# Seven experts' results leave by slot and come back by token: DRAM rows and indirect transfers in place of products with one-hot rows

## The chip, the core and the metric

The kernel runs on one core of a Trainium2 chip. The metric is the device time of one execution in microseconds, the median of several runs. The profile names the engines PE (TensorE; PEld is its weight load), DVE (VectorE), ACT (ScalarE), POOL (GpSimd) and SP (SyncE, which here only issues transfers).

## The reference

Two layers over 256 latent tokens of width 1024, with 256 context tokens beside them. Layer 0 is attention and a linear-attention group with a dense feed-forward block; layer 1 is neighbourhood attention and the mixture of experts that this change is about:

```python
def _moe(h, w_router, wg, wu, wd):
    logits = (h @ w_router).astype(jnp.float32)
    top_v, top_i = lax.top_k(logits, TOP_K)              # TOP_K = 2 of 8 experts
    gates = jax.nn.softmax(top_v, axis=-1)
    comb = jnp.sum(gates[..., None] * jax.nn.one_hot(top_i, N_EXPERTS), axis=-2)
    out = jnp.zeros_like(h)
    for e in range(N_EXPERTS):
        out = out + comb[..., e:e + 1] * _swiglu(h, wg[e], wu[e], wd[e])
    return out
...
        x = x + gt2 * ffn(_modulate(_rmsnorm(x, g_norm2[i]), sh2, sc2))
...
    return _rmsnorm(x, g_final)
```

Each expert has three float32 matrices of 1024 x 3584 (3 x 14.68 = 44.04 MB), so eight experts are 352.3 MB of weights for 512 token-expert pairs.

## The kernel before

Layer 0 and the attention of layer 1 take the first 1,040 us; they are not touched. Then the router gives each token two experts, a gate for each, and a rank among the tokens of that expert. Tokens are gathered into slots: an expert has `CAP` = 96 slots (three groups of 32), and a one-hot matrix `oh` (tokens by slots) turns the rows of `xr[2:4]` (the two tiles of 128 tokens) into `X_all` (features by slots), two experts at a time (`gather_pair`, tiles `gx`).

`run_experts` goes through 16 halves, two to an expert (n = 0 to 15; expert n // 2, half b = n % 2). A half is: `up`, the gate product `pg` (8 loads of 896 KB, 192 matmul instructions), then the up product `pu` (the same), then ACT's SiLU and DVE's product and transpose into `eT`; and behind that `down`, the product `py` of the half before (7 loads of 1 MB, 336 instructions). Every weight goes by `load_raw` on SP's queue into a ring of 13 buffers; SP may issue a load when PE has read the buffer out. `mm_quarters` spreads a product over four groups of 32 columns of PE, so that four matmuls run beside each other.

In the middle of each `pu` (at k = 4) `run_experts` calls `middle(n)`, which does two things. For an expert whose last `down` is over, that is at n = 3, 5, ... 15, it calls `scatter`: ACT and DVE copy `py` out of PSUM into `yF`, which is split into `yhi` and `ylo`; PE multiplies both by `ohT` (slots by tokens) into `sc`, eight matmuls of 96 x 512; DVE multiplies by the token's gate and by `gate2`, and POOL (DVE for the last expert) adds to `xr`. Then `between(n)` runs: at even n `route_slots` transposes the expert's one-hot matrix into `ohT` (two PE transposes and an ACT copy), at n = 2, 6, 10 the next pair is gathered, and at n = 0 `route_gates` makes the gates and counts tokens per expert. Expert 7's `scatter` stands behind everything, followed by `finish_out`, the final norm. Program order on each engine comes from a scheduler that follows priorities; weight loads stand 500 steps ahead.

Of the kernel before, what the change touches and what calls it, by code (L numbers as in the profile page):

```python
# [7 lines left out]
F32 = mybir.dt.float32  # L8
F32R = mybir.dt.float32r
I32 = mybir.dt.int32  # L10
AF = mybir.ActivationFunctionType
ALU = mybir.AluOpType
AX = mybir.AxisListType
# [3 lines left out]
P = 128  # L17
D = 1024
KT = 8
# [6 lines left out]
NE = 8  # L26

GROUPS = 3
CAP = 32 * GROUPS
# [10 lines left out]
C_W8 = C_WIN + 64  # L40
# [49 lines left out]
def kernel(ctx, tc, x, c, ctx_in, c_ctx, w_mod, b_mod, g_norm1, g_norm2, w_in_ab, g_q, g_k,  # L90
# [3 lines left out]
    nc = tc.nc  # L94
# [4 lines left out]
    def new_pool(stack, name, bufs=1, side="left", **kw):  # L99
        return stack.enter_context(tc.tile_pool(name=name, bufs=bufs, side=side, reuse_waits="tile", **kw))  # L100

    small = ctx.enter_context(tc.tile_pool(name="small", bufs=4))
    dram = ctx.enter_context(tc.tile_pool(name="dram", bufs=1, space=DRAM))
# [12 lines left out]
    def bankA(name):  # L116
        return banks["p"].tile([P, 512], F32, tag="p", name=name)

    def bankB(name, tag="x"):
        return banks[tag].tile([P, 512], F32, tag=tag, name=name)  # L120
# [23 lines left out]
    def cc(o, n=P):  # L144
        return cst[:, o - P:o - P + n] if o < C_KEEP else cst0[:, o - C_KEEP:o - C_KEEP + n]
# [13 lines left out]
    def pick(tags, n):  # L159
        seq = [t for t in tags for _ in range(t[2])]  # L160
        return seq[n % len(seq)]
# [66 lines left out]
    featp = new_pool(ctx, "featp", side="right")  # L228
# [104 lines left out]
    def gate_rows(pool, l, cond, v, tag, bufs, bank="x"):  # L333
        g = pool.tile([P, D], F32, tag=tag, bufs=bufs, name=f"gate{l}_{cond}_{v}")
        for h in range(2):
            q = 2 * v + h
            i, j = q // 4, q % 4
            ps = bankB(f"gate_ps{l}_{cond}_{v}_{h}", bank)
            sel = ident[:, 32 * j + cond:32 * j + cond + 1].to_broadcast([P, P])
            nc.tensor.matmul(ps, sel, m_sb[l][:, i, :], start=True, stop=True)  # L340
            nc.scalar.copy(g[:, h * 512:(h + 1) * 512], ps)
        return g
# [171 lines left out]
    with ahead(PREP):  # L514
        nz = state["n"]
        state["n"] += 1
        pool, tag, bufs = pick(raw_tags, state["r"])
# [4 lines left out]
        pool, tag, bufs = pick(hi_tags, nz)  # L522
        wz_hi = pool.tile([P, KT, P], F32R, tag=tag, bufs=bufs, name="wz_hi")
        pool, tag, bufs = pick(lo_tags, nz)
# [43 lines left out]
    for d in range(2):  # L568
        tri = cc(C_TF if d == 0 else C_TB)
        for p in range(2):  # L570
            ps = bankB(f"bc{d}_{p}")
            for t in range(NT):
                o = d * 256 + p * P
                nc.tensor.matmul(ps[:, t * P:(t + 1) * P], la[:, t, o:o + P], tri, start=True, stop=True)
            e1 = t1p.tile([P, 512], F32, tag="gt", bufs=3, name=f"e1_{d}_{p}")
            e2 = t1p.tile([P, 512], F32, tag="gt", bufs=3, name=f"e2_{d}_{p}")
# [151 lines left out]
    xr = [(resc if t < 2 else resid).tile([P, D], F32, name=f"xr{t}") for t in range(NT)]  # L728
# [228 lines left out]
    for g in range(NG):  # L957
# [27 lines left out]
        for t in range(NT):  # L985
            for half in range(2):
                hs = slice(half * 512, half * 512 + 512)
# [10 lines left out]
    for s, cond in streams:  # L998
        both = fmp.tile([P, 2, D], F32, tag=f"fT{s}", bufs=2, name=f"xc{s}")
# [29 lines left out]
    gate2 = gate_rows(resid, 1, 0, 5, "gate", 1, bank="s")  # L1029
# [97 lines left out]
    mop = new_pool(mo, "mop", side="right")  # L1127
# [6 lines left out]
    rank = mop.tile([P, 2, NE], F32, name="rank")  # L1134
    cnt_i = mop.tile([1, 1], I32, name="cnt_i")
    oh, ohT = {}, {}
# [4 lines left out]
    tops, scales = [], []  # L1141
# [3 lines left out]
    def rt(name, n=NE):  # L1145
        return mop.tile([P, n], F32, name=name)
# [78 lines left out]
    def route_rows():  # L1225

        for t in range(2):
            for h in range(2):
                hs = slice(h * 512, h * 512 + 512)
                nc.scalar.mul(xs_hi[t][:, hs], xr[2 + t][:, hs], scales[t])  # L1230
                scaled = exp_.tile([P, 512], F32, tag="ytmp", bufs=2, name=f"scaled{t}_{h}")
                nc.scalar.mul(scaled, xr[2 + t][:, hs], scales[t])
                nc.gpsimd.tensor_tensor(xs_lo[t][:, hs], scaled, xs_hi[t][:, hs].bitcast(F32), op=ALU.subtract)

    def one_hot(ep):

        oh[ep] = mop.tile([P, 2, 2, CAP], F32R, tag="oh", bufs=2, name=f"oh{ep}")
        for e in range(2):
            for t in range(2):
                nc.vector.tensor_scalar(oh[ep][:, t, e, :], iota, rank[:, t, 2 * ep + e:2 * ep + e + 1],  # L1240
                                        sel[:, t, 2 * ep + e:2 * ep + e + 1], op0=ALU.is_equal, op1=ALU.mult)

    def route_exp():
        for t in range(2):
# [3 lines left out]
            nc.scalar.activation(e2, e2, AF.Exp)  # L1248
            tops[t] += [e2]

    def route_gates():
        for t in range(2):
            m1, o1, m2, o2, e2 = tops[t]
            den, g1 = rt(f"den_{t}", 1), rt(f"g1_{t}", 1)
            nc.vector.tensor_scalar_add(den, e2, 1.0)
            nc.vector.reciprocal(g1, den)
            nc.vector.tensor_tensor(e2, e2, g1, op=ALU.mult)
            nc.vector.tensor_scalar_mul(o1, o1, g1)
            nc.vector.scalar_tensor_tensor(comb[:, t, :], o2, e2, o1, op0=ALU.mult, op1=ALU.add)
        ps = bankB("cnt_ps")  # L1260
        for t in range(2):
            nc.tensor.matmul(ps[:, 0:NE], cc(C_ONE), sel[:, t, :], start=(t == 0), stop=(t == 1))
        cmax = rt("cmax", 1)
        nc.vector.tensor_reduce(cmax, ps[:, 0:NE], axis=AX.X, op=ALU.max)
        nc.vector.tensor_copy(cnt_i, cmax[0:1, :])

    def slot_rows(ohs, name):

        tp = bankA(f"ohT_ps{name}").bitcast(F32R)
        for t in range(2):  # L1270
            nc.tensor.transpose(out=tp[0:CAP, t * P:(t + 1) * P], in_=ohs[t], identity=ident_r)
        rows_ = mop.tile([CAP, 256], F32R, tag="ohT", bufs=2, name=f"ohT{name}")
        nc.scalar.copy(rows_, tp[0:CAP, 0:256].bitcast(F32))
        return rows_

    def route_slots(e):
        ohT[e] = slot_rows([oh[e // 2][:, t, e % 2, :] for t in range(2)], f"{e}")
# [10 lines left out]
    NB, BW = 2, 1792  # L1288
# [28 lines left out]
    class Expert:  # L1317
# [41 lines left out]
        def down(self, b, eTs):  # L1359
# [4 lines left out]
            for i in range(ni):  # L1364
                with ahead(PREP):
                    wd = load_raw(self.wd[b * ni + i], [P, 2, D])
                for j in range(2):

                    begin = b == 0 and i == 0 and j == 0
                    for s in range(GROUPS):  # L1370
                        mm_quarters(self.py[s], eTs[s][:, 2 * i + j, :], wd[:, j].rearrange("p (q x) -> p q x", q=4),
                                    begin and s % 2 == 0, b == NB - 1 and i == ni - 1 and j == 1)

        def scatter(self):
            name, pool = self.name, self.pool
            ohT_e = self.ohT_e()
            yF = y_room()
            hi, lo = [pool.tile([CAP, D], F32R, tag=f"y{p}", bufs=1, name=f"y{p}_{name}") for p in ("hi", "lo")]
            pss = {}
            for h in range(2):  # L1380
                hs = slice(h * 512, h * 512 + 512)
                for n, (s, q) in enumerate((s, q) for s in range(GROUPS) for q in (2 * h, 2 * h + 1)):
                    (nc.vector.tensor_copy if n % 2 else nc.scalar.copy)(  # L1383
                        yF[32 * s:32 * s + 32, q * 256:(q + 1) * 256], self.py[s][32 * q:32 * q + 32])
                nc.scalar.copy(hi[:, hs], yF[:, hs])
                nc.vector.tensor_tensor(lo[:, hs], yF[:, hs], hi[:, hs].bitcast(F32), op=ALU.subtract)
                for t in range(2):
                    ps = bankA(f"sc_{name}_{h}_{t}")
                    for n, part in enumerate((hi, lo)):
                        nc.tensor.matmul(ps, ohT_e[:, t * P:(t + 1) * P], part[:, hs], start=(n == 0), stop=(n == 1))  # L1390
                    tmp = pool.tile([P, 512], F32, tag="ytmp", bufs=2, name=f"ytmp_{name}_{h}_{t}")
                    nc.vector.scalar_tensor_tensor(tmp, ps, self.gate(t), gate2[:, hs], op0=ALU.mult, op1=ALU.mult)  # L1392
                    (nc.vector if self.last else nc.gpsimd).tensor_tensor(xr[2 + t][:, hs], xr[2 + t][:, hs], tmp,  # L1393
                                                                          op=ALU.add)

    def run_experts(experts, between=lambda n: None):

# [23 lines left out]
    rooms = {}  # L1421

    def X_room(ep):

        if "X" not in rooms:
            rooms["X"] = featp.tile([P, 2, KT, 2 * CAP], F32, tag="f0", bufs=1, name="X_all")
        return rooms["X"][:, ep % 2]

    def y_room():

        if "y" not in rooms:
            both = featp.tile([P, D], F32, tag="f1", bufs=1, name="yF")
            rooms["y"] = both
        return rooms["y"][0:CAP]

    def gather_pair(ep, tags):
        rows, ohs = ((xs_hi, xs_lo), oh[ep]) if ep else ((xr[2:4],), oh_r)
# [3 lines left out]
    def between(n):  # L1441

        ep, i = divmod(n, 2 * NB)
        if n == 0:
            with tc.issue_after(critical["gathered"]), tc.issue_after(critical["one-hot"]):
                one_hot(0)
                route_gates()
                route_rows()
        if n % NB == 0:
            route_slots(n // NB)  # L1450
        if i == 1 and ep + 1 < NE // 2:
            with tc.issue_after(critical["one-hot"]):
                one_hot(ep + 1)
        if i == 2 and ep + 1 < NE // 2:
            gather_pair(ep + 1, "p")
# [98 lines left out]
```

## Time and profile before

| | |
|---|---|
| median of 3 runs | 1993.11 us (1990.57 to 1993.86) |
| the profiled execution's own time | 1991.23 us |
| its span, first to last instruction | 1989.3 us |
| PE busy | 1926.8 us (97%) |
| DVE, ACT, POOL busy | 741.6, 448.0, 142.7 us |
| moved by the DMA engines | 493.32 MB, mean 248 GB/s |

The span is what the views of the profile show; 1.9 us of the profiled time lie around it. A line number is that of the kernel before.

### The profile page before, as it was taken

What the parts mean: (1) busy time and instruction counts of PE and PEld (TensorE: products, weight loads), DVE (VectorE), ACT (ScalarE), POOL (GpSimd) and SP (SyncE); (2) the same over time, 40 slices, a digit from 0 to 9 for tenths busy, and PEclk for the clock granted to TensorE, in tenths of its full rate; (3) what the DMA queues carried; (4) which work ended last, traced back from release to release, by engine and by line L of the source; (5) the groups of instructions that cost most, each with busy time, mean ns of one, the idle gap of its engine ahead of it and who ended that gap; (6) DMA issues with size and microseconds to landing.
All of it is one profiled execution on the core that took longest, in us unless ns stands there. A gap on an engine that the chain in (4) does not pass through costs nothing.

```text
span 1989.3 us, 37121 instructions
## 1 busy us (share of the span) xinstructions
PE 1926.8 (97%) x16627; PEld 1177.0 (59%) x16627; DVE 741.6 (37%) x1190; ACT 448.0 (23%) x732; POOL 142.7 (7%) x177
## 2 busy tenths in 40 slices
PE   5999999899999999999999999999999999999996
PEld 3666676787878877777764444545444344544433
DVE  3246588866556435536772101011110101111022
ACT  4232165422222222336542010010100010010001
POOL 1101010100000000104211000001010100101010
PEclk8999999999999999999999999999999999999998
DMA  8624120634536244233239999999999999999991
GB/s 335 218 104 170 48 82 14 235 133 170 201 132 217 85 129 136 73 99 94 74 129 368 399 394 386 379 405 379 385 387 402 392 388 362 377 409 385 407 398 40
DMA packets 125213, 493.32 MB, mean 248 GB/s; under 512 B 10696, under 2 KB 58120, under 8 KB 104568
## 3 DMA queue, kind: packets, MB, share of 16 engines
q1 hardware_dynamic: 114096, 481.04, 63.6%
q10 hardware_dynamic: 8648, 6.48, 1.1%
q0 software_dynamic: 2304, 3.36, 0.8%
q8 instruction: 132, 2.16, 0.4%
q14 instruction: 33, 0.27, 0.0%
HBM read 486.13 MB, written 4.72 MB: 247 GB/s over the span
## 4 chain that ended last, share of the span: by engine, by line
PE 93%; DVE 2%; DMA 2%; ACT 1%; issue 1%; POOL 0%; SPq 0%; POOLq 0%; ACTq 0%; DVEq 0%
PE pu_e L1315 15%; PE pg_e L1315 15%; PE py_e L1315 15%; PE pf_fu L481 3%; PE pf_fu L482 3%; PE pf_fu L483 3%; PE pf_fg L481 3%; PE pf_fg L482 3%; PE pf_fg L483 3%; PE fd L217 3%; PE fd L215 2%; PE fd L216 2%; PE sc_e L1390 1%; PE mod_ps L254 1%; PE o_c L860 1%
## 5 line engine op out<-in xcount | busy, mean ns | idle before, releaser
L1315 PE MATMUL pu_e<-raw,X_all 128*32 128x448 f32 x3072 | 306.1, 540 | 0.0
L1315 PE MATMUL py_e<-raw,eT_e 128*32 128x256 f32 x5376 | 296.5, 379 | 0.0
L1315 PE MATMUL pg_e<-raw,X_all 128*32 128x448 f32 x3024 | 291.4, 539 | 0.0
L1315 PEld LDWEIGHTS py_e<-raw,eT_e 128*32 128x32 f32 x5376 | 190.5, 110 | 105.0 <-issue 5.1
L1315 PEld LDWEIGHTS pg_e<-raw,X_all 128*32 128x32 f32 x3024 | 100.0, 110 | 181.2 <-issue 175.5
L1315 PEld LDWEIGHTS pu_e<-raw,X_all 128*32 128x32 f32 x3072 | 98.5, 110 | 182.4 <-issue 178.8
L204 DVE TENSOR_TENSOR wlo<-raw,whi 128x2048 fp32r<-128x2048 f32 (+1 forms) x69 | 153.2, 2227 | 125.2 <-ACT whi L202 124.8
L202 ACT CAST whi<-raw 128x2048 fp32r<-128x2048 f32 (+1 forms) x73 | 135.1, 1859 | 267.0 <-PE fd L217 113.3
L1352 DVE TENSOR_TENSOR m_sb<-m_sb,pu_e 128x448 f32<-128x448 f32 x48 | 27.9, 604 | 393.5 <-PE pu_e L1315 393.4
L1348 ACT ACTIVATE m_sb<-pg_e 128x448 f32<-128x448 f32 x48 | 26.1, 544 | 512.8 <-PE pg_e L1315 512.8
L481 PE MATMUL pf_fu<-f_hi,whi 128*128 128x512 f32 (+1 forms) x240 | 91.5, 381 | 3.4 <-ACT whi L202 3.4
L1393 POOL TENSOR_TENSOR xr<-xr,ytmp_e 128x512 f32<-128x512 f32 x28 | 35.2, 1277 | 822.5 <-DVE ytmp_e L1392 822.5
L481 PE MATMUL pf_fg<-f_hi,whi 128*128 128x512 f32 (+1 forms) x240 | 93.0, 388 | 0.6 <-ACT whi L202 0.6
L483 PE MATMUL pf_fg<-f_hi,wlo 128*128 128x512 f32 (+1 forms) x240 | 91.6, 382 | 1.8 <-DVE wlo L204 1.8
L482 PE MATMUL pf_fg<-f_lo,whi 128*128 128x512 f32 (+1 forms) x240 | 92.2, 384 | 0.7 <-DVE f_lo L381 0.7
L482 PE MATMUL pf_fu<-f_lo,whi 128*128 128x512 f32 (+1 forms) x240 | 91.7, 382 | 0.0
L483 PE MATMUL pf_fu<-f_hi,wlo 128*128 128x512 f32 (+1 forms) x240 | 91.5, 381 | 0.0
L217 PE MATMUL fd<-whi,fT 128*128 128x512 f32 x224 | 88.3, 395 | 0.0
L215 PE MATMUL fd<-whi,fT 128*128 128x512 f32 x224 | 88.0, 393 | 0.0
L216 PE MATMUL fd<-wlo,fT 128*128 128x512 f32 x224 | 88.0, 393 | 0.0
L1392 DVE SCALAR_TENSOR_TENSOR ytmp_e<-sc_e,comb,gate 128x512 f32<-128x512 f32 x32 | 23.6, 750 | 165.3 <-PE sc_e L1390 160.5
L1383 ACT COPY yF<-py_e 32x256 f32<-32x256 f32 x48 | 17.4, 363 | 265.9 <-PE py_e L1315 257.6
(375 smaller groups left out, 2676.6 us busy)
## 6 DMA issues: line engine op xcount, KB each, us to landing
raw<-in_w_moe_up_dram SPq DMA_DIRECT2D x128, 896.0 KB, 6.4
raw<-in_w_moe_down_dram SPq DMA_DIRECT2D x112, 1024.0 KB, 8.0
raw<-in_w_moe_gate_dram SPq DMA_DIRECT2D x126, 896.0 KB, 7.8
raw<-in_w_mod_dram SPq DMA_DIRECT2D x48, 1024.0 KB, 4.9
raw<-in_w_ff_gate_dram SPq DMA_DIRECT2D x14, 1024.0 KB, 5.6
raw<-in_w_ff_up_dram SPq DMA_DIRECT2D x14, 1024.0 KB, 5.4
raw<-in_w_ff_down_dram SPq DMA_DIRECT2D x14, 1024.0 KB, 4.9
raw<-in_w_in_c_dram SPq DMA_DIRECT2D x12, 1024.0 KB, 5.2
```

The costliest lines, as they stand in the source:

```text
L202: nc.scalar.copy(hi[:, c], raw[:, c])
L204: low.tensor_tensor(lo[:, c], raw[:, c], hi[:, c].bitcast(F32), op=ALU.subtract)
L215: nc.tensor.matmul(ps, ah, bh, start=start, stop=False)
L216: nc.tensor.matmul(ps, ah, bl, start=False, stop=False)
L217: nc.tensor.matmul(ps, al, bh, start=False, stop=stop)
L481: nc.tensor.matmul(ps, wh[:, k, ws], hh[:, k, ts], start=(k == 0), stop=False)
L482: nc.tensor.matmul(ps, wh[:, k, ws], hl[:, k, ts], start=False, stop=False)
L483: nc.tensor.matmul(ps, wl[:, k, ws], hh[:, k, ts], start=False, stop=(k == KT - 1))
L1315: nc.tensor.matmul(out[32 * q:32 * q + 32], lhsT, rhs[:, q], start=start, stop=stop, skip_group_check=True)
L1348: nc.scalar.activation(g, ps[s][:, 0:QW], AF.Silu)
L1352: nc.vector.tensor_tensor(gs[s], gs[s], ps[s][:, 0:QW], op=ALU.mult)
L1393: (nc.vector if self.last else nc.gpsimd).tensor_tensor(xr[2 + t][:, hs], xr[2 + t][:, hs], tmp, op=ALU.add)
```

## The change

Experts 0 to 6 no longer multiply by `ohT`. `store` copies `py` into `yF` (one of two places, in turn), multiplies by `gate2`, and ACT issues a transfer of the 96 rows of 4 KB to their slots in a DRAM tensor `y_d` of 7 x 96 rows and one row of zeros. `route_back`, called from `route_gates`, works out for each token and each of its two choices the row in `y_d` (the zero row for expert 7 and for a token beyond the 96 slots). At n = 15 `add_back` has POOL issue four indirect transfers, each of 128 rows of 4 KB, one for each token tile and choice, into free parts of the tiles of `yF` and `X_all`, and DVE adds them to `xr` with the gates. Expert 7 keeps the product with `ohT`. `ohT` is made for expert 7 alone.

```diff
+    NY = (NE - 1) * CAP
+    y_d = dram.tile([NY + 1, D], F32, name="y_d")
+    y_idx = mop.tile([P, 2, 2], I32, name="y_idx")
+    def route_back():
+        zero = mop.tile([8, P], F32, name="zero")
+        nc.gpsimd.memset(zero, 0.0)
+        nc.scalar.dma_start(y_d[NY:NY + 1, :].rearrange("o (a b) -> (o a) b", a=8), zero)
+        for t in range(2):
+            v, u = rt(f"v{t}"), rt(f"u{t}")
+            nc.vector.scalar_tensor_tensor(v, cc(C_W8, 8), -float(CAP), rank[:, t, :], op0=ALU.mult, op1=ALU.add)
+            nc.vector.tensor_scalar_add(v, v, float(8 * CAP - NY))
+            nc.vector.scalar_tensor_tensor(v, rank[:, t, :], float(CAP), v, op0=ALU.is_lt, op1=ALU.mult)
+            nc.vector.memset(v[:, NE - 1:NE], 0.0)
+            for k in range(2):
+                i = rt(f"i{t}_{k}", 1)
+                nc.vector.tensor_tensor(u, v, tops[t][1 + 2 * k], op=ALU.mult)
+                nc.vector.tensor_reduce(i, u, axis=AX.X, op=ALU.add)
+                nc.vector.tensor_scalar_add(y_idx[:, t, k:k + 1], i, float(NY))
+    def add_back():
+        rooms_ = [rooms["y"][:, 2], rooms["y"][:, 3], rooms["X4"][:, 0:D], rooms["X4"][:, 3 * D:4 * D]]
+        for t in range(2):
+            for k in range(2):
+                nc.gpsimd.indirect_dma_start(rooms_[2 * t + k], None, y_d,
+                                             bass.IndirectOffsetOnAxis(ap=y_idx[:, t, k:k + 1], axis=0))
+        for t in range(2):
+            m1, o1, m2, o2, e2, g1 = tops[t]
+            for h in range(2):
+                hs = slice(h * 512, h * 512 + 512)
+                for k, g in enumerate((g1, e2)):
+                    xh = xr[2 + t][:, hs]
+                    nc.vector.scalar_tensor_tensor(xh, rooms_[2 * t + k][:, hs], g, xh, op0=ALU.mult, op1=ALU.add)
     def route_gates():
+        route_back()
...
+        def store(self):
+            n = int(self.name[1:])
+            yF = y_room(n % 2)
+            for h in range(2):
+                hs = slice(h * 512, h * 512 + 512)
+                for i, (s, q) in enumerate((s, q) for s in range(GROUPS) for q in (2 * h, 2 * h + 1)):
+                    (nc.vector.tensor_copy if i % 2 else nc.scalar.copy)(
+                        yF[32 * s:32 * s + 32, q * 256:(q + 1) * 256], self.py[s][32 * q:32 * q + 32])
+                nc.vector.tensor_tensor(yF[:, hs], yF[:, hs], gate2[0:CAP, hs], op=ALU.mult)
+            nc.scalar.dma_start(y_d[n * CAP:n * CAP + CAP, :], yF)
         def scatter(self):
+            if not self.last:
+                return self.store()
...
-        if n % NB == 0:
-            route_slots(n // NB)
+        if n == (NE - 1) * NB:
+            route_slots(NE - 1)
+        if n == NE * NB - 1:
+            add_back()
```

The scheduler's order shows what this does to the engines. The first place is PE in the middle of expert 1's second half (n = 3), where expert 0 is scattered; `pu_e_1` is the up product, `sc` the product with `ohT`. Before:

```order
L1315 MATMUL pu_e_1_9146<-raw_9190,X_all 32x448 x4
L1315 MATMUL pu_e_1_9147<-raw_9190,X_all 32x448 x4
L1390 MATMUL sc_e_0_0_9215<-yhi_e_9205,ohT_8052 128x512 [waits Activation_49]
L1390 MATMUL sc_e_0_0_9215<-ylo_e_9206,ohT_8052 128x512 [waits DVE_49]
L1390 MATMUL sc_e_0_1_9221<-yhi_e_9205,ohT_8052 128x512 [waits Activation_49]
L1390 MATMUL sc_e_0_1_9221<-ylo_e_9206,ohT_8052 128x512
L1390 MATMUL sc_e_1_0_9235<-yhi_e_9205,ohT_8052 128x512 [waits Activation_49]
L1390 MATMUL sc_e_1_0_9235<-ylo_e_9206,ohT_8052 128x512 [waits DVE_49]
L1315 MATMUL pu_e_1_9145<-raw_9247,X_all 32x448 [waits DMAHW3_49]
L1390 MATMUL sc_e_1_1_9241<-yhi_e_9205,ohT_8052 128x512 [waits DVE_49]
L1390 MATMUL sc_e_1_1_9241<-ylo_e_9206,ohT_8052 128x512
L1315 MATMUL pu_e_1_9145<-raw_9247,X_all 32x448 x3
```

And in the changed kernel, from the same weight tile on:

```order
L1354 MATMUL pu_e_1_9169<-raw_9199,X_all 32x448 x4
L1354 MATMUL pu_e_1_9170<-raw_9199,X_all 32x448 x4
L1354 MATMUL pu_e_1_9168<-raw_9213,X_all 32x448 [waits DMAHW4_49]
L1354 MATMUL pu_e_1_9168<-raw_9213,X_all 32x448 x3
L1354 MATMUL pu_e_1_9169<-raw_9213,X_all 32x448 x4
```

The eight products are gone and the up product runs through; the next weight tile comes on semaphore lane 4 in place of 3, since the store to `y_d` has taken lane 3.

The second place is DVE in the last half (n = 15), between the end of expert 6 and the product `m_sb` that makes expert 7's last `eT`. Before:

```order
L1386 TENSOR_TENSOR ylo_e_14694<-yF,yhi_e_14693 96x512 [waits Activation_49]
L1392 SCALAR_TENSOR_TENSOR ytmp_e_0_0_14706<-sc_e_0_0_14703,comb,gate_0_5_6114 128x512 [waits PE_49,Pool_49]
L1392 SCALAR_TENSOR_TENSOR ytmp_e_0_1_14712<-sc_e_0_1_14709,comb,gate_0_5_6114 128x512 [waits PE_49,Pool_49]
L1392 SCALAR_TENSOR_TENSOR ytmp_e_1_0_14726<-sc_e_1_0_14723,comb,gate_0_5_6114 128x512 [waits PE_49,Pool_49]
L1392 SCALAR_TENSOR_TENSOR ytmp_e_1_1_14732<-sc_e_1_1_14729,comb,gate_0_5_6114 128x512 [waits PE_49,Pool_49]
L1352 TENSOR_TENSOR m_sb_1588<-m_sb_1588,pu_e_1_14634 128x448 [waits PE_49,Activation_49]
```

In the changed kernel:

```order
L1422 TENSOR_TENSOR yF<-yF,gate_0_5_6114 96x512 [waits DVE_49]
L1286 SCALAR_TENSOR_TENSOR xr_1594<-yF,g_0_8047,xr_1594 128x512 [waits DMASW0_49]
L1286 SCALAR_TENSOR_TENSOR xr_1594<-yF,g_0_8047,xr_1594 128x512
L1286 SCALAR_TENSOR_TENSOR xr_1594<-yF,e_0_7831,xr_1594 128x512 [waits DMASW1_49,DVE_49]
L1286 SCALAR_TENSOR_TENSOR xr_1594<-yF,e_0_7831,xr_1594 128x512 [waits DVE_49]
L1286 SCALAR_TENSOR_TENSOR xr_1595<-X_all,g_1_8054,xr_1595 128x512 [waits DMASW2_49]
L1286 SCALAR_TENSOR_TENSOR xr_1595<-X_all,g_1_8054,xr_1595 128x512
L1286 SCALAR_TENSOR_TENSOR xr_1595<-X_all,e_1_7834,xr_1595 128x512 [waits DMASW3_49,DVE_49]
L1286 SCALAR_TENSOR_TENSOR xr_1595<-X_all,e_1_7834,xr_1595 128x512 [waits DVE_49]
L1391 TENSOR_TENSOR m_sb_1588<-m_sb_1588,pu_e_1_14470 128x448 [waits PE_49,Activation_49]
```

DVE now waits for the four indirect transfers (the lanes DMASW0 to DMASW3) ahead of the work that makes `eT`. The third place is POOL's issue of them, behind the last work that POOL has from the start of the expert stage:

```order
L1233 TENSOR_TENSOR xs_lo_7644<-scaled_1_8079,xs_hi_7642 128x512 [waits Activation_49]
L1278 DMA yF<-y_d,y_idx 128x1024 [waits DMAHW4_49,DMAHW3_49,DMAHW5_49,DMAHW2_49,DMAHW6_49,DMAHW1_49,DMAHW7_49,DVE_49,PE_49]
L1278 DMA yF<-y_d,y_idx 128x1024 [waits DVE_49]
L1278 DMA X_all<-y_d,y_idx 128x1024 [waits PE_49,Activation_49]
L1278 DMA X_all<-y_d,y_idx 128x1024 [waits DVE_49]
L349 TENSOR_TENSOR rs_nf_fin<-ms_nf_fin,mhalf 128x1 [waits DVE_49] x2
```

The 28 additions to `xr` that stood here on POOL are gone; the first transfer waits for the stores of all seven experts, the third also for PE, which reads `X_all`.

## Rows read from the trace of the kernel before

**Rows 1.** The page: busy us by engine, and DMA busy tenths in 40 slices.

```profile
PE 1926.8 (97%) x16627; PEld 1177.0 (59%) x16627; DVE 741.6 (37%) x1190; ACT 448.0 (23%) x732; POOL 142.7 (7%) x177
...
DMA  8624120634536244233239999999999999999991
```

**Rows 2.** First and last matmuls of the expert stage, line 1315 (ns, then start us).

```profile
L1315 PE MATMUL py_e<-raw,eT_e x5376: 379/379/379, 1133.4 to 1967.7; 128*32 128x256 f32 x200
...
L1315 PE MATMUL pg_e<-first,X_all x48: 539/539/563, 1060.0 to 1064.1; 128*32 128x448 f32 x48
```

**Rows 3.** The chain in order of time, halves n = 4 and 5 (start, us, what).

```profile
1267.89 0.20 PE pg_e L1315
...
1268.11 17.66 PE pg_e L1315 x187
...
1295.17 0.27 PE ohT_ps L1271 x2
...
1304.59 18.13 PE py_e L1315 x336
1322.72 18.04 PE pg_e L1315 x192
...
1380.19 4.87 PE pg_e L1315 x49
```

**Rows 4.** The chain in order of time, half n = 9.

```profile
1550.50 18.04 PE pg_e L1315 x192
1568.54 0.67 PE sc_e L1390 x2
...
1608.25 18.04 PE pg_e L1315 x192
```

**Rows 5.** Stretches of the expert stage: busy time by engine, clock, DMA.

```profile
core 0: us, PE busy (x) PEld busy (x) DVE busy (x) ACT busy (x) POOL busy (x), PEclk, DMA share, GB/s
...
1452.00:1465.00 13.00, 13.00 (x144) 4.42 (x136) 0.00 (x0) 1.63 (x3) 0.00 (x0) 1.00 1.01 423
...
1100.00:1930.00 830.00, 830.00 (x10592) 373.21 (x10588) 96.89 (x177) 61.05 (x132) 35.25 (x28) 1.00 1.00 390
```

**Rows 6.** What SP's queue waited for in the expert stage (total us, times, longest).

```profile
SPq L169 <- PE pu_e L1315: 263.4, 121, 5.9
SPq L169 <- PE pg_e L1315: 243.5, 124, 16.7
SPq L169 <- PE py_e L1315: 215.5, 99, 2.2
```

**Rows 7.** What PE's weight loads waited for: the costliest wait for a transfer.

```profile
PEld pu_e L1315 <- DMA raw<-in_w_moe_down_dram: 2.0, 8, 0.2
```

**Rows 8.** SP's timeline: when the seven loads used from 1304.59 are issued.

```profile
1277.18 13.86 SPq L169 DMA_DIRECT2D raw<-in_w_moe_down_dram  x7
```

**Rows 9.** DMA issues by line: KB each, median us to landing.

```profile
raw<-in_w_moe_down_dram SPq DMA_DIRECT2D x112, 1024.0 KB, 8.0
...
bias<-rb_d POOLq DMA_DIRECT2D x32, 96.0 KB, 2.9
...
out_dram<-z_fin ACTq DMA_DIRECT2D x2, 256.0 KB, 2.5
```

**Rows 10.** DVE's timeline in the last half, n = 15.

```profile
1892.20 1.77 DVE L1383 COPY yF<-py_e 32x256 f32<-32x256 f32 x4 [16.11 <-ACT yF L1383]
...
1896.77 0.69 DVE L1386 TENSOR_TENSOR ylo_e<-yF,yhi_e 96x512 fp32r<-96x512 f32 x1 [0.69 <-ACT yhi_e L1385]
...
1919.67 0.75 DVE L1392 SCALAR_TENSOR_TENSOR ytmp_e<-sc_e,comb,gate 128x512 f32<-128x512 f32 x1 [2.30 <-PE sc_e L1390]
...
1930.41 0.62 DVE L1352 TENSOR_TENSOR m_sb<-m_sb,pu_e 128x448 f32<-128x448 f32 x1 [6.93 <-PE pu_e L1315]
...
1932.67 1.16 DVE L1354 STREAM_TRANSPOSE eT_e<-m_sb 128x448 f32<-128x448 f32 x2
```

**Rows 11.** The chain in order of time, the end of the expert stage.

```profile
1931.78 35.87 PE py_e L1315 x664
```

More of the change, by code (lines that the diff above doesn't have):

```diff
@@ L1257, in route_gates @@
             nc.vector.tensor_tensor(e2, e2, g1, op=ALU.mult)
+            tops[t] += [g1]
             nc.vector.tensor_scalar_mul(o1, o1, g1)
@@ L1271, in slot_rows @@
             nc.tensor.transpose(out=tp[0:CAP, t * P:(t + 1) * P], in_=ohs[t], identity=ident_r)
-        rows_ = mop.tile([CAP, 256], F32R, tag="ohT", bufs=2, name=f"ohT{name}")
+        rows_ = mop.tile([CAP, 256], F32R, tag="ohT", bufs=1, name=f"ohT{name}")
         nc.scalar.copy(rows_, tp[0:CAP, 0:256].bitcast(F32))
@@ L1392, in scatter @@
                     nc.vector.scalar_tensor_tensor(tmp, ps, self.gate(t), gate2[:, hs], op0=ALU.mult, op1=ALU.mult)
-                    (nc.vector if self.last else nc.gpsimd).tensor_tensor(xr[2 + t][:, hs], xr[2 + t][:, hs], tmp,
-                                                                          op=ALU.add)
+                    nc.vector.tensor_tensor(xr[2 + t][:, hs], xr[2 + t][:, hs], tmp, op=ALU.add)
     def run_experts(experts, between=lambda n: None):
@@ L1425, in X_room, with y_room @@
         if "X" not in rooms:
-            rooms["X"] = featp.tile([P, 2, KT, 2 * CAP], F32, tag="f0", bufs=1, name="X_all")
+            rooms["X4"] = featp.tile([P, 4 * D], F32, tag="f0", bufs=1, name="X_all")
+            rooms["X"] = rooms["X4"][:, 0:4 * KT * CAP].rearrange("p (a k n) -> p a k n", a=2, k=KT)
         return rooms["X"][:, ep % 2]
-    def y_room():
+    def y_room(i=0):
         if "y" not in rooms:
-            both = featp.tile([P, D], F32, tag="f1", bufs=1, name="yF")
-            rooms["y"] = both
-        return rooms["y"][0:CAP]
+            rooms["y"] = featp.tile([P, 4, D], F32, tag="f1", bufs=1, name="yF")
+        return rooms["y"][0:CAP, i]
     def gather_pair(ep, tags):
```

## The prediction

> **What bounds the kernel now.** I read the page first. PE is busy for 1926.8 us of the span [rows 1], so time can only go where PE gets less to do, unless something stands close behind it. Something does: the DMA tenths read 9 through the whole second half [rows 1]. That half is the expert stage, which the change touches, from PE's first `pg` at 1060.0 to its last `py` at 1967.7 [rows 2]: 907.7 us. So the question is whether PE or the weight stream paces it.
>
> The stretches say both are full: from 1100 to 1930 PE is busy for 830.00 of 830 us at the full clock and the DMA share is 1.00, at 390 GB/s [rows 5]. A share of 1.00 does not yet make a limit, for in the stretch from 1452 to 1465 us, where SP issues faster than usual, a share of 1.01 stands beside 423 GB/s [rows 5]; 390 is what is asked of the DMA engines, not what they can do. Two more views tell the same. SP's queue spent 722 us waiting for PE to read buffers out (263.4, 243.5 and 215.5) [rows 6], while PE's costliest wait for a weight load is 2.0 us in all, in eight pieces [rows 7]. And the seven loads whose first use is at 1304.59 [rows 3] are issued from 1277.18 on [rows 8]: 27.4 us ahead, of which landing takes about 8.0 [rows 9], so that a weight lies ready for some 19 us. PE paces the stage; the stream follows it with 19 us in hand.
>
> **What a half costs without anything in its middle.** The chain gives 18.04 us for 192 gate matmuls and 18.13 us for 336 `py` [rows 3]; the up product has as many matmuls of the same shape as the gate product, 18.04. A bare half is 54.21 us, and 16 of them 867.4. The stage takes 907.7, so 40.3 us are for what stands between: scatters, `ohT`, the gathers, the count.
>
> **Removed: seven scatters.** Half n = 5 holds one and nothing else. It runs from 1322.72 to 1380.19 [rows 3], 57.47 us. At such a seam two gate matmuls of the next half run before the last `py` (one of the two pieces stands at 1267.89); at 18.04/192 = 0.094 us each they belong to the other half: 57.28, or 3.07 over the bare half. Half n = 9 runs from 1550.50 to 1608.25 [rows 4], 57.75: 3.54 over. There the scheduler put the products one or two at a time between up matmuls ([rows 4] shows two `sc` in front), and each change of shape costs. In the chain n = 3, 5, 7 and 11 have the first form, n = 9, 13 and 15 the second: 4 x 3.07 + 3 x 3.54 = 22.9 us. Bounds: the first form throughout gives 21.5, the second 24.8.
>
> **Removed: seven transpositions into `ohT`.** Half n = 4 has one alone: from 1268.11, less 0.19 for its two early gate matmuls, to 1322.72 [rows 3] is 54.80, 0.59 over. At n = 8 and 12 it is the same. At n = 0, 2, 6 and 10 a count or a gather stands beside it and pays for the change of shape anyway; there only its own 0.27 [rows 3] goes. 3 x 0.59 + 4 x 0.27 = 2.9. Together 25.8 us. The rest of the 40.3, 14.5 us, is left to what stays (three gathers, the count, expert 7's `ohT`).
>
> **Removed elsewhere.** 28 additions on POOL, 28 gated products on DVE, the splits into `yhi` and `ylo` on ACT and DVE: none is on the path, since PE is busy throughout [rows 5]. I price them at nothing. Expert 7's own scatter and the final norm, the time after 1967.7, are unchanged.
>
> **Added at the start: `route_back`.** Twenty DVE operations of a few elements, a memset, one small transfer that ACT issues. They stand under expert 0's gate product, when DVE has nothing PE waits for before the first half's end. Nothing.
>
> **Added: seven stores.** ACT issues one after DVE's second product with `gate2`; behind it on ACT is the SiLU of the same half. At n = 15 the copies run from 1892.20 and the second 96 x 512 operation that now becomes that product starts at 1896.77 and takes 0.69 [rows 10], so the store goes at about 1897.5. The SiLU needs the gate product, which lasts 18.04 us from about 1892: 13 us of cover. The store takes a semaphore lane from the weight loads; SP waits for it eight loads later, some 18 us after. Landing: between 2.5 us (256 KB, ACT's queue) and 8.0 (1024 KB under the weight stream) [rows 9]. Hidden either way.
>
> **Added: traffic.** Seven stores of 0.39 MB and four fetches of 0.52 MB are 4.85 MB. From 1100 to 1930 the engines moved 390 x 0.830 = 323.7 MB; nearly all of the change's gain lies there, so the same work and 4.85 MB more would have to pass in about 805 us: 408 GB/s, against 423 seen [rows 5]. The 19 us in hand are worth 7.8 MB at that rate, so PE starts to wait only if the sustained rate falls below (328.5 - 7.8)/805 = 398 GB/s. Below that, each per cent costs 8 us. I take 423, the row that shows a full queue, and so nothing.
>
> **Added: the fetch and eight additions at n = 15.** POOL's first fetch waits for the last store, landed between 1900 and 1905.5. A fetch of 512 KB has no row; its bounds are 2.9 us (96 KB on POOL's queue) and 8.0 (1024 KB) [rows 9], so four, one after the other at worst, end between 1912 and 1938; if the last two wait for the up matmuls ahead of them on PE, they still start by about 1920. Eight additions of 128 x 512 at 0.75 each [rows 10] are 6 us: done between 1918 and 1944. DVE has the product `m_sb` next, which ran at 1930.41, its transposes ending at 1933.8 [rows 10]. PE uses that `eT` only after expert 7's first `py`: 1931.78 + 18.13 [rows 11, 3], less the 3.54 that this half loses, 1946.4. DVE must therefore begin by 1943. Against the early bound there are 25 us to spare, against the late one 1 us is missing. I take the early side (nearer in size and with overlap between fetches): nothing.
>
> **The sum.** 25.8 us off the profiled execution's 1991.23 gives 1965.4; off the median 1993.11, which is 1.9 higher, 1967.3. I say 1967, and for this case 1963 to 1971 (scatters 21.5 to 24.8, transpositions 1.9 to 4.1, and the 3.3 us spread of the runs).
>
> **Rivals.** (1) *The weight stream was the limit all along.* Then PE's gaps closed nothing, since the share of 1.00 says the engines are full; the 4.85 MB come on top at 390 GB/s, 12.4 us: **2005**, slower. For it: the share [rows 5]. Against it: 423 GB/s and the waits of [rows 6, 7]. It decides if 390 is a limit, that is if SP stops waiting for PE.
> The Trainium skill speaks for this rival: "DMA: Bandwidth & Descriptors", Specifications, gives a limit of about 358 GB/s for HBM per core. By it 328.5 MB need 918 us, 88 more than before, and the kernel would end near 2081. This trace does not agree, with 390 GB/s over 830 us [rows 5].
> (2) *The stream becomes the limit once PE is quicker*, since stores between loads cost more than their bytes. At a sustained 390 after the change, (328.5 - 7.8)/390 = 822 us in place of 805: 17 of the 25.8 us are given back, **1985**. At 386 all of them, and below that the kernel is slower than before. For it: 408 of 423 leaves 3.5%. Against it: a small store every 108 us is 0.9% of the bytes.
> (3) *The fetch is late and DVE holds back the last `eT`.* PE then stands still before expert 7's last `py`. Each us past 1943 costs one; at 10 us past, **1977**. It outweighs the gain only if the additions end after 1969, 71 us after the store is issued.
> (4) *The gaps go only in part*: PE's removed products leave a wait in their place, as PSUM banks now turn over in another order and a gate product meets a SiLU or eviction that it used to follow. Half the gain, **1980**. Against it: evictions are done 5 us after `py` [rows 10], half a half ahead of need.
>
> **Chances.** Forecast 0.80; rival (1) 0.04, (2) 0.07, (3) 0.05, (4) 0.04. The range for 8 in 10 is 1962 to 1977: the forecast's own range with a us on the low side, and upwards to the mild ends of (2), (3) and (4). 0.2%, or 4 us, is about what a measurement of this kernel tells from no change. Rivals (2) and (3) reach no change or worse in a third of their weight, (1) is slower: faster 0.91, same 0.03, slower 0.06.
>
> **What would show it.** In the changed kernel's chain a half with nothing in it takes 54.2 us, seven more of them than now; SP still waits mostly for PE; the DMA rate from 1100 to the end of the stage is about 405 GB/s; PE has no wait for a transfer above a few us; DVE's additions end before 1943 on the old scale (about 1918 on the new); and the tail after the last `py` is as long as before. I am wrong if PE waits for weights in growing pieces towards the end, if it stands before the last `py`, or if bare halves take longer than 54.2.

## The result and the profile after

The changed kernel takes 1966.57 us (median of 4 runs, 1965.11 to 1969.37) against 1992.38 for the kernel before in the same call: a ratio of 0.9872, with a 95% interval of 0.986 to 0.9885 (estimated from all runs; it need not be the quotient of the two medians to the last digit). The profiled execution took 1966.8 us, with a span of 1964.9.

The page of the changed kernel, as [rows 1]: busy us by engine, and the DMA busy tenths.

```profile
PE 1903.2 (97%) x16557; PEld 1171.3 (60%) x16557; DVE 726.8 (37%) x1190; ACT 437.5 (22%) x711; POOL 111.6 (6%) x154
...
DMA  9634020645436343123337999999999999999994
```

PE lost 23.6 of its busy us and is still the engine that never rests; every DMA slice that lies wholly in the expert stage still reads 9. The chain in order of time, halves n = 4 and 5, a piece of n = 6, and the end, as [rows 3, 11]:

```profile
1264.43 18.04 PE pg_e L1354 x192
...
1318.64 18.04 PE pg_e L1354 x192
...
1372.85 18.04 PE pg_e L1354 x192
1390.89 2.25 PE pu_e L1354 x24
1393.43 2.39 PE pu_e L1354 x24
1396.11 2.39 PE pu_e L1354 x24
1398.79 2.39 PE pu_e L1354 x24
1401.18 3.42 PE gx L1342 x29
...
1431.88 18.04 PE pg_e L1354 x192
...
1907.37 35.93 PE py_e L1354 x666
```

Half n = 4 (1264.43 to 1318.64) and half n = 5 (to 1372.85) last 54.21 us each: bare, as the prediction priced them. The last `py` instruction begins at 1943.3, and the span ends 21.6 us later, as before (1989.3 less 1967.7).

SP's queue, what it waited for most between 1060 and 1945 us (us in total, times, longest), as [rows 6]; then the weight loads of PE, as [rows 7]:

```profile
SPq L169 <- PE pu_e L1354: 228.2, 118, 5.8
SPq L169 <- PE py_e L1354: 190.6, 92, 2.2
SPq L169 <- PE pg_e L1354: 188.7, 103, 14.4
SPq L169 <- DMA y_d<-yF: 63.8, 6, 14.8
SPq L169 <- DMA raw<-in_w_moe_down_dram: 22.6, 18, 2.9
```
```profile
PEld pg_e L1354 <- DMA raw<-in_w_moe_up_dram: 2.9, 12, 0.2
```

SP now waits for the stores too: 63.8 us in six pieces, up to 14.8. PE's own worst wait for a weight is still 0.2 us. The DMA issues by line (KB each, median us to landing), as [rows 9]:

```profile
raw<-in_w_moe_down_dram SPq DMA_DIRECT2D x112, 1024.0 KB, 12.9
...
y_d<-yF ACTq DMA_DIRECT2D x7, 384.0 KB, 5.1
...
yF<-y_d,y_idx POOLq DMA_INDIRECT x2, 10.5
X_all<-y_d,y_idx POOLq DMA_INDIRECT x2, 15.3
```

And DVE's timeline in the last half, as [rows 10]:

```profile
1891.52 1.42 DVE L1286 SCALAR_TENSOR_TENSOR xr<-yF,g,xr 128x512 f32<-128x512 f32 x2 [15.98 <-DMA yF<-y_d,y_idx]
...
1902.94 1.41 DVE L1286 SCALAR_TENSOR_TENSOR xr<-X_all,e,xr 128x512 f32<-128x512 f32 x2 [3.08 <-DMA X_all<-y_d,y_idx]
1906.06 0.62 DVE L1391 TENSOR_TENSOR m_sb<-m_sb,pu_e 128x448 f32<-128x448 f32 x1 [1.71 <-PE pu_e L1354]
```

The additions end at 1904.35, and `m_sb` behind them waits for PE, not for them.

### The profile page after: what moved, and what is told of

Same layout as the page of the kernel before. It is cut to its first block, busy times and chain, and to the rows that moved or that the text cites. A ratio compares the mean times of both kernels' runs of the same rounds, so it can differ in the third digit from the quotient of the medians.

```text
span 1964.9 us, 36952 instructions
## 1 busy us (share of the span) xinstructions
PE 1903.2 (97%) x16557; PEld 1171.3 (60%) x16557; DVE 726.8 (37%) x1190; ACT 437.5 (22%) x711; POOL 111.6 (6%) x154
## 4 chain that ended last, share of the span: by engine, by line
PE 93%; DVE 2%; DMA 2%; ACT 2%; issue 1%; POOL 0%; SPq 0%; ACTq 0%; POOLq 0%; DVEq 0%
PE pu_e L1354 15%; PE py_e L1354 15%; PE pg_e L1354 15%; PE pf_fu L481 3%; PE pf_fu L482 3%; PE pf_fu L483 3%; PE pf_fg L481 3%; PE pf_fg L482 3%; PE pf_fg L483 3%; PE fd L217 3%; PE fd L216 3%; PE fd L215 3%; PE mod_ps L254 1%; PE o_c L860 1%; PE gx L1342 1%
## 5 line engine op out<-in xcount | busy, mean ns | idle before, releaser
L1354 PE MATMUL pu_e<-raw,X_all 128*32 128x448 f32 x3072 | 296.2, 539 | 0.0
L1420 DVE COPY yF<-py_e 32x256 f32<-32x256 f32 x42 | 17.7, 421 | 116.4 <-ACT yF L1420 115.8
L736 DVE TENSOR_TENSOR rtmp_ff<-fd,gate 128x512 f32<-128x512 f32 x56 | 38.7, 691 | 40.7 <-PE fd L217 39.2
```

Of the source, the lines that this page charges most:

```text
L736: nc.vector.tensor_tensor(tmp, ps, gate[:, hs], op=ALU.mult)
L1354: nc.tensor.matmul(out[32 * q:32 * q + 32], lhsT, rhs[:, q], start=start, stop=stop, skip_group_check=True)
L1420: (nc.vector.tensor_copy if i % 2 else nc.scalar.copy)(yF[32 * s:32 * s + 32, q * 256:(q + 1) * 256], self.py[s][32 * q:32 * q + 32])
```

## The experiments

The theory is that the gain is PE's time for the 56 products and the transpositions; the stores, the fetch and the additions are covered, the stores by the lead of the weights. The rivals are the prediction's, and one that the trace after adds: SP's 63.8 us of waiting cost part of the gain.

Medians of whole runs scatter by 2 us, since the stage begins anywhere from 1058.5 to 1062.5 us. Each run therefore also has the stage's length in its profile, from the start of the first `pg` to the start of the last `py` instruction. Four kernels with the changed kernel's PE products (a_pool_store, a_no_traffic, a_pool_4x, a_late12) agree there within 0.01 us, at 882.96 and 882.97. The changed kernel's own profile reads 0.28 more. All of it lies in one instruction: the last four `py`, which run beside each other, begin 882.96 us behind the first `pg` in it and 882.94 to 882.95 in the others, but the last of the four starts 0.30 us behind the first in it and 0.02 in the others. Why is open; 882.97 is the figure to compare with.

| run | median us | ratio to before, 95% | stage us |
|---|---|---|---|
| before | 1992.38 | | 907.69 |
| after | 1966.57 | 0.9872, 0.986 to 0.9885 | 883.25 |
| b_no_scatter | 1968.41 | 0.9884, 0.9868 to 0.9901 | 884.37 |
| a_ohT_all | 1968.33 | 0.9885, 0.9868 to 0.9901 | 884.36 |
| a_pool_store | 1967.12 | 0.9875, 0.9859 to 0.9892 | 882.97 |
| a_no_traffic | 1965.66 | 0.9874, 0.9858 to 0.9891 | 882.97 |
| a_act_4x | 1972.19 | 0.9905, 0.9888 to 0.9921 | 888.81 |
| a_pool_4x | 1966.02 | 0.9873, 0.9856 to 0.9889 | 882.96 |
| a_late12 | 1967.45 | 0.9879, 0.9862 to 0.9895 | 882.97 |
| a_late20 | 1975.65 | 0.9923, 0.9906 to 0.9939 | 893.41 |
| a_late32 | 1993.84 | 1.0009, 0.9999 to 1.0019 | 909.80 |
| a_gather_hi | 1963.86 | 0.9867, 0.985 to 0.9883 | 880.54 |

**b_no_scatter: the removal alone.** In the kernel before, behind the split into `yhi` and `ylo`:

```diff
+                if not self.last:
+                    continue
                 for t in range(2):
                     ps = bankA(f"sc_{name}_{h}_{t}")
```

> The kernel before, without the scatter's products for experts 0 to 6: their 56 products of py's kind with a one-hot row each, the gated copy behind them and the addition into the tokens are left out, so the output lacks those seven experts; the transpositions of ohT, the weights and every load stay, and there is no store and no fetch. Theory (the products' time on TensorE is what the change takes away): 22.9 us less than before, with the bounds of the prediction 21.5 to 24.8, so about 1969.5 and between 1967.6 and 1970.9. Rival (the gain comes from VectorE and ScalarE work, or from the ohT transpositions): less than 15 us off. Rival (a faster TensorE runs into the weight stream, and the change paid for that with its stores): more than 25 us off, below 1967.

Measured: the stage is 23.3 us shorter (907.69 to 884.37), where 22.9 was expected. Its first `pg` and its last `py`, in the form of [rows 2]:

```profile
L1315 PE MATMUL py_e<-raw,eT_e x5376: 379/379/379, 1133.8 to 1944.8; 128*32 128x256 f32 x200
...
L1315 PE MATMUL pg_e<-first,X_all x48: 539/539/563, 1060.4 to 1064.6; 128*32 128x448 f32 x48
```

The removal, with no store and no fetch in the kernel, gives nearly the whole gain. The `continue` also leaves out the gated copies on DVE and the additions on POOL. PE was busy for 805.00 of the 805 us from 1100 to 1905 before and is so here, so the stage is as long as PE's own work, and the gain is that of the products.

**a_ohT_all: the transpositions put back.**

```diff
-        if n == (NE - 1) * NB:
-            route_slots(NE - 1)
+        if n % NB == 0:
+            route_slots(n // NB)
```

> The changed kernel with one part undone: ohT is made again for all eight experts, though only expert 7's is used. Theory: the transpositions stand in TensorE's own row of work, three at 0.59 us and four at 0.27 us, so 2.9 us more than the changed kernel, about 1969.5. Rival (TensorE has slack because the weight stream limits): no more than 0.5 us. Together with the run without the scatter's products this gives the whole difference as 22.9 + 2.9.

Measured: 1.4 us longer than the kernels at 882.97 (884.36; 1.1 longer than the changed kernel's own profile), where 2.9 was expected. The sign is the theory's, the size is not. PE has the same products here as in b_no_scatter, with the stores, the fetch and the additions on top, and the stages are 884.36 and 884.37: the traffic costs nothing beside them. The chain of this kernel, halves n = 4 and 6:

```profile
1265.04 18.04 PE pg_e L1354 x192
...
1319.65 18.04 PE pg_e L1354 x192
...
1373.86 18.04 PE pg_e L1354 x192
1391.90 6.77 PE pu_e L1354 x72
1399.09 2.39 PE pu_e L1354 x24
1401.48 3.64 PE gx L1342 x31
...
1414.27 18.13 PE py_e L1354 x336
```

Half n = 4, with a transposition alone, lasts 1319.65 - 1265.04 = 54.61, 0.40 over a bare half and not 0.59. Half n = 6, with a transposition beside a gather, lasts 1414.27 + 18.13 - 1373.86 = 58.54; without the transposition, in the changed kernel, it lasts 1431.88 - 1372.85 = 59.03. Taking it away there costs half a us: the scheduler now cuts the up product four times, three times for a single gather product and then for the other 29 (the four pieces of 24 in the chain after), where with the transposition there are two cuts, and one of them holds the transposition as well. Half by half the transposition costs 0.40 at n = 0, 4, 8 and 12 and 0.14 at n = 2 and 10, and it saves 0.49 at n = 6: 1.39 in all.

**a_pool_store and a_no_traffic: the cover.** In the first, GpSimd issues the stores; in the second the stores, the fetches and the additions are gone.

```diff
-            nc.scalar.dma_start(y_d[n * CAP:n * CAP + CAP, :], yF)
+            nc.gpsimd.dma_start(y_d[n * CAP:n * CAP + CAP, :], yF)
```

> The changed kernel with the seven stores issued on GpSimd's queue in place of ScalarE's; nothing else. The trace of the changed kernel shows SP held 63.8 us in six waits for those stores. Theory (each hold is shorter than the lead of the weights, so it costs nothing): the same time, 1966.6 within 1 us, though SP's wait for the stores goes to nothing and the loads of the last expert come again about 20 us ahead of their use in place of 8. Rival (the holds cost part of the gain): 3 to 10 us faster than the changed kernel, near 1960.

> The changed kernel without the seven stores, the four fetches and the additions; the output lacks experts 0 to 6. Theory (all of it lies beside TensorE's products): 1966.6 within 1 us. Rival (the 4.85 MB of traffic or the late fetch costs time): 5 to 12 us faster, near 1957 by 4.85 MB at about 400 GB/s. What would speak against both is a slower run.

Measured: both stages last 882.97. Neither SP's waits nor 4.85 MB nor the fetch cost PE time; the 0.28 us of the last instruction are all that the changed kernel's profile has on top. In a_pool_store the wait for `y_d` is gone from SP's list:

```profile
SPq L169 <- PE pu_e L1354: 247.1, 126, 5.8
SPq L169 <- PE pg_e L1354: 243.9, 125, 15.6
SPq L169 <- PE py_e L1354: 215.4, 99, 2.2
```

The last update of a load's semaphore tells when it landed; what lies between that and the first product that uses it is its lead. The shortest lead among an expert's loads, in us, for experts 0 to 7:

| run | lead by expert |
|---|---|
| before | 18.7, 19.0, 20.2, 19.8, 20.4, 19.1, 19.3, 20.1 |
| after | 18.7, 18.2, 13.4, 14.2, 11.2, 12.1, 10.8, 3.5 |
| a_pool_store | 18.6, 18.4, 17.6, 17.7, 18.5, 18.0, 17.9, 13.9 |
| a_no_traffic | 18.8, 18.6, 19.1, 19.2, 19.0, 18.7, 19.0, 19.7 |
| a_act_4x (below) | 18.5, 14.7, 9.1, 7.2, 2.3, 3.4, 1.3, 0.0 |

The 20 and 8 us of the expectation, and the 8 to 20 us of a_act_4x's, are from a count of bytes, which reads 4 to 6 us too much; the last expert's lead came back to 13.9 and not to 20. So the change's traffic costs no time, but with the stores on ScalarE's queue it takes all of the 19 us except 3.5.

**a_act_4x and a_pool_4x: bytes or waits.** Three more stores behind each, from ScalarE in the first run, and all four from GpSimd in the second:

```diff
             nc.scalar.dma_start(y_d[n * CAP:n * CAP + CAP, :], yF)
+            for c in range(3):
+                nc.scalar.dma_start(y_c[c * NY + n * CAP:c * NY + n * CAP + CAP, :], yF)
```

> The changed kernel with every store issued four times from ScalarE, three of them into a spare DRAM tensor that nothing reads: 8.3 MB more of writes. By the bytes alone the stage needs about 421 GB/s in place of 408, still under the 423 that one window of the kernel before shows: at most 3 us more, 1967 to 1970. If a store on ScalarE's queue holds SP's loads for as long as it is outstanding, four of them hold it at four loads in a row, the lead of 8 to 20 us is used up each time, and TensorE waits: 1975 to 1985, with SP's wait for the stores well above 63.8 us.

> The same four stores in each place issued on GpSimd's queue. The bytes are the same as in the run from ScalarE, but no load of SP should wait for a store. If bytes are what costs, the time is that of the run from ScalarE; if the holding of SP is what costs there, this run stays at 1967 to 1970.

Measured: 5.8 us more in the stage from ScalarE, nothing from GpSimd, with the same bytes. So it is not the bytes: the run from GpSimd moved 411 GB/s from 1100 to 1905 us, and PE did not wait (columns as in [rows 5]):

```profile
1100.00:1905.00 805.00, 805.00 (x10517) 352.15 (x10513) 79.30 (x151) 50.88 (x112) 17.97 (x32) 1.00 1.01 411
```

The run from ScalarE moved 404 and has the wait in its chain, at the last of the seven stores:

```profile
1852.74 17.74 PE py_e L1355 x328
1877.03 10.58 DMA y_c<-yF
1887.67 15.37 DMA raw<-in_w_moe_up_dram
1903.08 4.72 PE pu_e L1355 x48
```
```profile
1889.77 2.46 PE L1355 MATMUL pu_e<-raw,X_all 128*32 128x448 f32 x24 [0.85 <-DMA raw<-in_w_moe_up_dram]
...
1903.08 9.46 PE L1355 MATMUL pu_e<-raw,X_all 128*32 128x448 f32 x96 [0.36 <-DMA raw<-in_w_moe_up_dram]
```

A store from ScalarE ends at 1887.61; only then does SP issue a load of `up`, and PE waits for that load's landing at 1903.04. It is the last of five such waits of PE in this up product, 4.3 us in all. Between the start of this half's gate product and the start of `py` lie 41.90 us (1870.69 to 1912.59), against 36.08 in the changed kernel, which is the whole 5.8. The size was less than the 8 to 18 us expected, and SP's wait for `y_d` did not grow (64.3 us, with 15.1 more for `y_c`). At the six stores before that PE did not wait, since some lead was left. But the lead fell over the stage (last row of the table), since between two rounds of stores the stream regained less than a round took.

**a_late12, a_late20, a_late32: the fetch made late.** GpSimd adds zeros to the last fetched tile 12, 20 or 32 times, ahead of VectorE's last additions:

```diff
+        zl = xs_lo[0][:, 0:512].bitcast(F32)
+        nc.gpsimd.memset(zl, 0.0)
+        late = rooms_[3][:, 0:512]
+        for _ in range(12):
+            nc.gpsimd.tensor_tensor(late, late, zl, op=ALU.add)
```

> The changed kernel with the last fetched rows delayed: behind the fetches GpSimd adds zeros twelve times to the first half of the last fetched tile, at about 1.28 us each, so that VectorE's last additions come about 15 us later, near 1920; the result is unchanged. Theory (fetch and additions have about 15 to 19 us to spare before TensorE wants the last expert's first activations near 1925): no cost, or no more than 2 us, 1966.6 to 1968.5. Rival (VectorE's order is already on the path): 10 to 15 us more.

> The same with 32 additions of zeros, about 41 us, so that VectorE's last additions end near 1945 and the first activations of the last half come about 1947, some 21 us after TensorE wants them. Theory (past the spare time each us late costs one, as in the prediction's third rival): about 21 us more, 1983 to 1991. Rival (TensorE can go on with other work): much less.

> The last fetched rows delayed by 20 additions of zeros, some 27 us. In the run with 32 TensorE stood idle for 23.9 us and the stage grew by 26.8: its last addition ended 887.3 us behind the first gate product, and the activations would have been wanted 1.4 us behind an addition that ended at 863.8. With 20 it should end at 871.0, so 7.2 us late. Theory (each us past the spare time costs one): the stage grows by 7 to 8 us from 883.0, 1974 to 1975. If a shorter idle stretch also makes the granted clock fall, as the run with 32 shows it behind 23.4 us without work (0.62 between 1949 and 1955 us), up to 3 us come on top: 1977 to 1978. Rival (the 26.8 us of the run with 32 have another cause than the wait): no fixed relation to the 7.2 us.

Measured: nothing with 12, whose last addition ended at 1921.79; 26.8 us more in the stage with 32, where about 21 were expected (the median, 1993.84, lies above the expected 1983 to 1991), and 10.4 more with 20. DVE and PE with 32 (a last bracket is the idle time ahead and what ended it):

```profile
1945.60 0.75 DVE L1291 SCALAR_TENSOR_TENSOR xr<-X_all,e,xr 128x512 f32<-128x512 f32 x1 [41.60 <-POOL X_all L1284]
```
```profile
1914.63 9.68 PE L1359 MATMUL py_e<-raw,eT_e 128*32 128x256 f32 x176
1947.74 1.08 PE L1359 MATMUL py_e<-raw,eT_e 128*32 128x256 f32 x8 [23.43 <-DVE eT_e L1398]
1949.33 19.95 PE L1359 MATMUL py_e<-raw,eT_e 128*32 128x256 f32 x328 [0.51 <-DVE eT_e L1398]
```

PE stands from 1924.31 to 1947.74, and begins again 1.39 us after the last addition ends at 1946.35. An addition that ended at 1922.9 would have been in time. With the 0.51 us that follow, PE's idle time explains 23.9 of the 26.8 us; the rest is the clock, read from two stretches of the same kernel (columns as in [rows 5]):

```profile
1926.00:1947.00 21.00, 0.00 (x0) 0.00 (x0) 1.37 (x2) 0.00 (x0) 18.48 (x15) 0.59 0.35 147
1949.00:1955.00 6.00, 5.67 (x68) 2.76 (x72) 0.80 (x2) 0.00 (x0) 0.00 (x0) 0.62 0.02 4
```

While PE stood still the granted clock fell to 0.59, a mean over stretches at the two levels (1.2 and 2.4 GHz), and it was 0.62 for the first 6 us of work. With 20 additions PE stood still for 8.0 us, and the next stretches read

```profile
1925.00:1931.00 6.00, 0.00 (x0) 0.00 (x0) 1.50 (x3) 0.00 (x0) 4.17 (x4) 0.60 1.02 426
1931.00:1937.00 6.00, 4.92 (x52) 2.03 (x56) 2.63 (x5) 0.00 (x0) 0.00 (x0) 0.54 0.33 135
```

so 2.4 of its 10.4 us are clock as well. Its median, 1975.65, lies just above the simple theory's 1974 to 1975; the stage tells the two apart.

**a_gather_hi: still less work for PE.**

```diff
-        rows, ohs = ((xs_hi, xs_lo), oh[ep]) if ep else ((xr[2:4],), oh_r)
+        rows, ohs = ((xs_hi,), oh[ep]) if ep else ((xr[2:4],), oh_r)
```

> The changed kernel with less work on TensorE: the gathers of the three later pairs of experts take only the high half of the rows, so half of their 96 one-hot products go (the low half of those rows is left out of the computation). Those products take 12.5 us in the changed kernel. Theory (TensorE is still the limit, and the weights still come early enough): 6.2 us less, near 1960.4. Rival (the weight stream, at 399 GB/s over the stage, is now the limit): no more than 1 us off, with waits for the loads on TensorE in place of the products.

Measured: 2.4 us less against the kernels at 882.97, a miss for both sides. The timeline of PE and of ScalarE at the last gather says why:

```profile
1620.19 0.91 PE L1342 MATMUL gx<-oh,xs_hi 128*128 128x192 f32 x6
1621.26 1.27 PE L1342 MATMUL gx<-oh,xs_hi 128*128 128x192 f32 x6 [0.16 <-ACT X_all L1344]
```
```profile
1620.69 2.52 ACT L1344 ACTIVATE X_all<-gx,mT,A 128x192 f32<-128x192 f32 x6 [2.28 <-PE gx L1342]
```

With two products to a block of features instead of four, PE meets ScalarE's copy (2.52/6 = 0.42 us a block, against 0.22 for two products) and the changes of shape stay. The whole 2.4 us lie in the three halves with a gather. So the run asks less of the weight stream than was meant, and still PE waited for no load above 0.2 us. But the lead of the last expert's loads shrank to 1.6 us, and SP's wait for the stores grew to 84.1 us: with the stores on ScalarE's queue the stream is close behind PE.

## Why the prediction was right, step by step

- **PE paces the stage: shown.** Taking PE's products away, with the copies and additions that hang on them, gives 23.3 us (b_no_scatter); taking the traffic away gives nothing (a_no_traffic). Rival (1) has fallen, and rival (2) for the bytes: 411 GB/s over 805 us with 8.3 MB more cost nothing, where it saw a limit at 390. What rival (2) says of stores between loads, that they cost more than their bytes, holds for the lead (19 us down to 3.5), and for the time once there are four times as many (a_act_4x). The Trainium skill's "HBM Reference", Specifications (TRN2), says that a core which streams alone measures well above its share of about 358 GB/s; the 411 agree with that, and not with the 358 as a limit.
- **Scatters, 22.9 forecast: 23.3.** Inside the bounds of 21.5 to 24.8.
- **`ohT`, 2.9 forecast: 1.4.** This is the term that was mis-sized, and its lower bound, 1.9, did not hold. Of the 0.59 for one alone, 0.19 belonged to the scatter in the half ahead: with the scatters gone a half with only the transposition costs 0.40. Beside a gather the forecast of 0.27 took the schedule as fixed; it changed, and at n = 6 the half grew. The forecast from the profiled execution, 1965.4, was 1.4 us below the profiled 1966.8: that is this term, 1.5 too large, and the 0.28 of the last instruction, less the 0.4 that the scatters gave more. That the median came out closer (1967 forecast, 1966.57 measured) is luck: runs scatter by more than that.
- **Stores, "SP waits for it eight loads later, some 18 us after. Hidden either way": the outcome right, the step wrong.** It counted from the store's issue, but SP runs ahead of PE by more than 20 us ([rows 8] against [rows 3]). The load eight places on reaches the lane before the store is issued at all: at expert 6, SP issued one load at 1865.98, ACT the store at 1875.61, and SP the next load, by its order the one on the store's lane, only at 1881.22. That makes 63.8 us in six waits. It cost nothing because there was lead enough for all the waits together, not because the store had landed by then. The prediction held the 19 us in hand against a low rate only and took none of them for the stores; 3.5 were left, so this "nothing" was near its edge. a_act_4x shows the price once the lead is gone.
- **Rate, about 405 GB/s forecast: 398.** That is the forecast's own threshold, below which PE starts to wait, and not the 423 that it took. Of the 8 MB that are missing against 408 some 6 are lead drawn down (15.5 us of lead at 0.4 MB a us, an estimate). Without the stores on ScalarE's queue the same stretch moved 403 (a_pool_store).
- **Fetch, each 2.9 to 8.0 us: 10.5 and 15.3.** Outside the bounds singly, but the four overlap: issued within 4.9 us from 1882.08, all landed by 1902.94, 20.9 us for all. The additions ended at 1904.35. This half starts 21.1 us earlier than before (1871.10 against 1892.17 in the chains), so that is 1925.4 on the old scale, within 1918 to 1944.
- **Rival (3), a us for each us late: right in kind, with a later threshold and a dearer slope.** The additions must end by about 863.8 us behind the first `pg`, which is 1923.9 in the changed kernel, not 1918. For its 1918 the prediction took some 25 us off 1943, from which this half's own 3.54 was already gone; the 21.1 us by which the half starts earlier give 1921.9. The other 2.0 are that PE begins with the first of three pieces of `eT`, 1.39 us behind the additions, where the prediction waited 3.4 us for all of them. That leaves 19.6 us to spare. Past it the clock adds 2.4 to 2.9 us.
- **Rival (4):** fallen for the scatters; halves are bare at 54.21. Its mechanism, another order that gives part back, is what was seen at n = 6, at half a us.

## What to carry to other kernels

Where one engine never rests and all else is covered, the price of a change is that engine's own seams, read by the half with and without the piece, and not the instruction's duration; but a piece that stands beside others must be priced with the order that it leaves behind. A small store put on a queue that shares its completion lanes (the semaphores that tell of a landing) with the main load stream is paid from the lead of that stream even when it costs no time; on GpSimd's queue it left most of the lead (17.6 us or more up to expert 6, against 10.8) at the same speed. An unchanged time does not show how near the edge it is, so read the lead as well. Before a transfer is called hidden, work out when the engine that would use its result is next in need, and test the margin by making it late.

## What was not expected of the hardware

- A store on ScalarE's queue held SP's loads for up to 14.8 us, though it landed in 5.1 (median): most of the longest hold, up to the issue at 1875.61, passed before the store was issued. The same store on GpSimd's queue took 8.0 to land and held none.
- Four indirect fetches of 128 rows of 4 KB each took 0.94 to 1.08 us apiece of POOL to issue and 20.9 us together to land under the weight stream, about 100 GB/s.
- The DMA engines sustained 411 GB/s for 805 us beside a PE at its full clock (a_pool_4x).
- The granted clock fell in a pause of PE of 8.0 us as in one of 23.9 (0.60 and 0.59 over the stretches shown); they cost 10.4 and 26.8 us.
